# Splitting one 912-column load of a ReLU row-sum kernel into 112 + 8 + 8 partitions

## The chip, the cores and the metric

The kernel runs on one core of one Trainium2 chip. The metric is device time in microseconds (us). The kernel before takes 160.81 us (median of 6 runs, 160.70 to 160.96). A program on one core shows no second core to compare with, so I rely on repeated runs; every run quoted here was classed fast and the granted clock was 1.0.

## The reference

```python
x = np.random.randn(32, 512, 1024).astype(np.float32)
relu_x = np.maximum(x, 0)
return np.sum(relu_x, axis=-1).astype(np.float32)
```

That is 16,384 rows of 1,024 floats, 67.1 MB read once, and 16,384 sums written.

## The kernel before

Each of the 128 partitions takes 128 rows. Seven large chunks of 16 rows rotate through three buffers; then come 8, 4 and 2 rows, and the last two rows in pieces. ACT applies ReLU, DVE sums, and near the end both do ReLU and sum in one instruction each. All loads are issued by SP on one queue. The end of the load is cut into four transfers so that little computing is left after the last byte:

```python
CUT = 912
HEAD = 256
# ...
    rows = xv[-1].rearrange("p j d -> p (j d)")[:, r * D : (r + 2) * D]
    flat = buf[:, tb, r : r + 2, :].rearrange("p j d -> p (j d)")
    first, second, third = [(0, CUT), (D + D // 2, 2 * D), (D + HEAD, D + D // 2)]
    for k, (lo, hi) in enumerate((first, second, third)):
        sp.dma_start(out=flat[:, lo:hi], in_=rows[:, lo:hi]).then_inc(
            s_in[NBIG + len(TAIL) + k], 16
        )
    sp.dma_start(out=seam[:, 2 : 2 + w + HEAD], in_=rows[:, CUT : D + HEAD]).then_inc(s_seam, 16)
# ...
    lo, hi = first
    act.wait_ge(s_in[-3], 16)
    dve.wait_ge(s_in[-3], 16)
    on_act(flat[:, lo : CUT // 2], seam[:, 0:1]).then_inc(s_half, 1)
    on_dve(flat[:, CUT // 2 : hi], seam[:, 1:2]).then_inc(s_half, 1)
# ... then second (ACT), third (DVE), and the seam with the partial sums (both)
```

I call these four transfers the first piece (912 columns), the second (512), the third (256) and the seam (368). The result goes out after the last pair of instructions on the seam.

Of the kernel before, what the change touches and what calls it, by code (L numbers as in the profile page):

```python
# [3 lines left out]
P = 128  # L4
# [7 lines left out]
TAIL = [8, 4, 2]  # L12
CUT = 912
HEAD = 256


def bass_relu_sum_kernel(
# [21 lines left out]
    NBIG = len(CHUNKS)  # L39
# [12 lines left out]
    w = D - CUT  # L52
    seam = nc.alloc_sbuf_tensor("seam", [P, 2 + w + HEAD + 2], fp32)
    res = nc.alloc_sbuf_tensor("res", [P, J], fp32)
# [3 lines left out]
    s_in = [nc.alloc_semaphore(f"s_in{i}") for i in range(n_in)]  # L58
# [11 lines left out]
    sp, act, dve = nc.sync, nc.scalar, nc.vector  # L70
# [14 lines left out]
    for c in range(NBIG + 1):  # L85
        if c >= NB:
            sp.wait_ge(s_dve, done[c - NB])
        if c < NBIG:
            i = 0
            for g, j, n in CHUNKS[c]:  # L90
                sp.dma_start(  # L91
                    out=buf[:, c % NB, i : i + n, :], in_=xv[g][:, j : j + n, :]
# [15 lines left out]
    rows = xv[-1].rearrange("p j d -> p (j d)")[:, r * D : (r + 2) * D]  # L108
    flat = buf[:, tb, r : r + 2, :].rearrange("p j d -> p (j d)")
    first, second, third = [(0, CUT), (D + D // 2, 2 * D), (D + HEAD, D + D // 2)]  # L110
    for k, (lo, hi) in enumerate((first, second, third)):
        sp.dma_start(out=flat[:, lo:hi], in_=rows[:, lo:hi]).then_inc(  # L112
            s_in[NBIG + len(TAIL) + k], 16
        )
    sp.dma_start(out=seam[:, 2 : 2 + w + HEAD], in_=rows[:, CUT : D + HEAD]).then_inc(s_seam, 16)
    sp.wait_ge(s_turn, 1)
    sp.dma_start(
        out=of[0:P].rearrange("(k q) -> k q", q=32), in_=turned[0:P:32, 0:32]
# [7 lines left out]
    def on_act(t, acc):  # L126
        return act.activation(t, t, AF.Relu, accum_out=acc)  # L127

    def on_dve(t, acc):
        return dve.tensor_scalar(  # L130
            out=t, in0=t, scalar1=0.0, scalar2=None, op0=ALU.max, op1=ALU.add, accum_out=acc
        )
# [4 lines left out]
    k = 0  # L137
    for c in range(NTWO):
# [17 lines left out]
        for n in DVE_STEPS[c]:  # L156
            if ready[r + n - 1] > seen:
# [3 lines left out]
                out=res[:, c * BIG + r : c * BIG + r + n],  # L161
                in_=buf[:, c % NB, r : r + n, :],
# [22 lines left out]
            f(buf[:, tb, i, :], res[:, j0 + i : j0 + i + 1])  # L185

    lo, hi = first
    act.wait_ge(s_in[-3], 16)
    dve.wait_ge(s_in[-3], 16)
    on_act(flat[:, lo : CUT // 2], seam[:, 0:1]).then_inc(s_half, 1)  # L190
    on_dve(flat[:, CUT // 2 : hi], seam[:, 1:2]).then_inc(s_half, 1)
    k = 2 + w
    lo, hi = second
    act.wait_ge(s_in[-2], 16)
    on_act(flat[:, lo:hi], seam[:, k + HEAD : k + HEAD + 1]).then_inc(s_seam, 1)
    lo, hi = third
    dve.wait_ge(s_in[-1], 16)
    on_dve(flat[:, lo:hi], seam[:, k + HEAD + 1 : k + HEAD + 2]).then_inc(s_seam, 1)
    act.wait_ge(s_seam, 16 + 2)
    act.wait_ge(s_half, 2)  # L200
    on_act(seam[:, 0:k], res[:, J - 2 : J - 1]).then_inc(s_last, 1)
    dve.wait_ge(s_seam, 16 + 2)
    on_dve(seam[:, k : k + HEAD + 2], res[:, J - 1 : J]).then_inc(s_last, 1)

# [33 lines left out]
```

## Time and profile before

| | kernel before |
|---|---|
| median of 6 runs | 160.81 us |
| span of the profiled run | 159.4 us |
| DMA engines' share of the time, 20 to 120 us | 1.00 |
| bytes read | 67.11 MB |
| packet of 3,648 B (one row of the first piece) | 142 ns, one every 0.139 us |
| last landing of first piece, second, third, seam | 155.93, 156.63, 156.99, 157.44 us |
| start of the last pair of instructions | 157.47 us |

A transfer does not land at one time: the trace has 16 semaphore updates for each of these transfers, and from 153 to 157 us their packets run in 16 trains side by side, so I count one update from each DMA engine. A wait ends with the last of them (DVE's wait for the third piece at 157.01 us, the last landing at 156.99). The lines of the profile, and how I read them, are in the prediction.

### The profile page before, as it was taken

Reading aid. Unit: us, or ns where it says so; the run is one execution under the profiler, and the core shown is the slowest. Engines: PE = TensorE matmul, PEld = TensorE weight load, DVE = VectorE, ACT = ScalarE, POOL = GpSimd, SP = SyncE. Lnnn points to the kernel's source line nnn. Section 1 sums busy time; section 2 is a strip of 40 time slices with the busy share of each in tenths; the row PEclk is TensorE's granted clock in tenths of the full one; section 3 lists DMA queues with packets and bytes.
Section 4 is the critical chain, followed back from the end, with each engine's and each line's share of the span. In section 5 each row is a group of like instructions: output and inputs, shape, how many; then the busy total and the mean of one; then the engine's idle time right before and its main releaser. Section 6 shows DMA issues by size and latency. Waiting matters only on the chain.

```text
span 159.4 us, 150 instructions
## 1 busy us (share of the span) xinstructions
DVE 120.6 (76%) x59; ACT 101.5 (64%) x54; POOL 0.2 (0%) x4
## 2 busy tenths in 40 slices
DVE  0000000009999999999999999999999999898995
ACT  3000059980799708996099941999329980496975
POOL 0000000000000000000000000000000000000000
DMA  9997996996996997989979969969969979798994
GB/s 378 493 401 339 493 526 263 526 526 263 526 493 296 526 444 345 526 378 411 526 312 477 526 263 526 526 263 526 526 263 526 444 345 526 321 469 374 417 400 142
DMA packets 2457, 67.18 MB, mean 421 GB/s; under 512 B 536, under 2 KB 792, under 8 KB 1176
## 3 DMA queue, kind: packets, MB, share of 16 engines
q1 hardware_dynamic: 2456, 67.18, 98.1%
q14 instruction: 1, 0.01, 0.0%
HBM read 67.11 MB, written 0.07 MB: 421 GB/s over the span
## 4 chain that ended last, share of the span: by engine, by line
DVE 55%; DMA 34%; ACT 9%; SPq 2%; issue 0%
DVE res L160 54%; DMA buf<-in_x_dram 34%; ACT buf L145 9%; SPq L101 1%; SPq L112 1%; DVE buf L130 0%; DVE seam L130 0%; SPq L91 0%; DVE turned L169 0%
## 5 line engine op out<-in xcount | busy, mean ns | idle before, releaser
L160 DVE TENSOR_REDUCE res<-buf 128x4 f32<-128x4096 f32 (+3 forms) x18 | 99.4, 5596 | 35.5 <-ACT buf L145 35.5
L145 ACT ACTIVATE buf<-buf 128x7168 f32<-128x7168 f32 (+5 forms) x13 | 80.4, 6233 | 46.1 <-DMA buf<-in_x_dram 46.1
L127 ACT ACTIVATE buf<-buf 128x1024 f32<-128x1024 f32 (+2 forms) x19 | 19.0, 999 | 8.9 <-DMA buf<-in_x_dram 8.9
L130 DVE TENSOR_SCALAR_CACHE_REDUCE buf<-buf 128x1024 f32<-128x1024 f32 (+2 forms) x19 | 20.7, 1143 | 1.7 <-DMA buf<-in_x_dram 1.6
L127 ACT ACTIVATION_READ_ACCUMULATOR buf<-buf 128x1 f32 x19 | 3.6, 188 | 0.0
L145 ACT ACT_TABLE_LOAD x1 | 1.3, 1283 | 1.3 <-PEq L223 1.3
L130 DVE DVE_READ_ACCUMULATOR buf<-buf 128x1 f32 x19 | 1.6, 84 | 0.0
L130 DVE TENSOR_SCALAR_CACHE_REDUCE seam<-seam 128x258 f32<-128x258 f32 x1 | 0.4, 421 | 0.0
L127 ACT ACTIVATE seam<-seam 128x114 f32<-128x114 f32 x1 | 0.3, 300 | 0.1
L169 DVE STREAM_TRANSPOSE turned<-res 128x32 f32<-128x32 f32 x1 | 0.2, 211 | 0.0
L127 ACT ACTIVATION_READ_ACCUMULATOR seam<-seam 128x1 f32 x1 | 0.2, 186 | 0.0
L223 POOL MEMSET const-bfloat16-1.0<- 128x1 bf16 x1 | 0.1, 101 | 0.0
L223 POOL MEMSET const-uint8-127<- 128x1 uint8 x1 | 0.1, 101 | 0.0
L223 POOL MEMSET const-float32-0.0<- 128x1 f32 x1 | 0.1, 98 | 0.2 <-issue 0.2
L223 POOL MEMSET const-float32-1.0<- 128x1 f32 x1 | 0.1, 98 | 0.0
L130 DVE DVE_READ_ACCUMULATOR seam<-seam 128x1 f32 x1 | 0.1, 82 | 0.0
## 6 DMA issues: line engine op xcount, KB each, us to landing
buf<-in_x_dram SPq DMA_DIRECT2D x1, 7680.0 KB, 21.1
buf<-in_x_dram SPq DMA_DIRECT2D x1, 4096.0 KB, 25.3
buf<-in_x_dram SPq DMA_DIRECT2D x1, 2048.0 KB, 29.9
buf<-in_x_dram SPq DMA_DIRECT2D x1, 1024.0 KB, 31.9
buf<-in_x_dram SPq DMA_DIRECT2D x1, 512.0 KB, 3.3
buf<-in_x_dram SPq DMA_DIRECT2D x1, 456.0 KB, 32.5
buf<-in_x_dram SPq DMA_DIRECT2D x1, 256.0 KB, 32.7
seam<-in_x_dram SPq DMA_DIRECT2D x1, 184.0 KB, 32.6
```

Of the source, the lines that this page charges most:

```text
L101: sp.dma_start(out=buf[:, tb, r : r + n, :], in_=xv[-1][:, r : r + n, :]).then_inc(s_in[NBIG + i], 16)
L112: sp.dma_start(out=flat[:, lo:hi], in_=rows[:, lo:hi]).then_inc(s_in[NBIG + len(TAIL) + k], 16)
L127: return act.activation(t, t, AF.Relu, accum_out=acc)
L130: return dve.tensor_scalar(out=t, in0=t, scalar1=0.0, scalar2=None, op0=ALU.max, op1=ALU.add, accum_out=acc)
L145: act.activation(t, t, AF.Relu).then_inc(s_act, 1)
L160: dve.tensor_reduce(out=res[:, c * BIG + r : c * BIG + r + n], in_=buf[:, c % NB, r : r + n, :], axis=X, op=ALU.add,).then_inc(s_dve, 1)
L169: dve.transpose(out=turned[:, :], in_=res[:, 0:32]).then_inc(s_turn, 1)
L223: nc = _bacc.Bacc("TRN2", target_bir_lowering=False, num_devices=1)
```

## The change

The intent: eight of the engines finish earlier than the other eight (the first piece's eighth landing at 155.68 us, the last at 155.93), so let the early ones carry part of the late ones' rows. The large transfer puts 7 rows on each of sixteen engines and the small ones one row each on eight: eight engines carry 9 rows and eight carry 7, where each carried 8. The wait is for 48.

```diff
+SHARES = [(0, 112), (112, 120), (120, 128)]
...
     for k, (lo, hi) in enumerate((first, second, third)):
-        sp.dma_start(out=flat[:, lo:hi], in_=rows[:, lo:hi]).then_inc(
-            s_in[NBIG + len(TAIL) + k], 16
-        )
+
+        for a, b in SHARES if k == 0 else [(0, P)]:
+            sp.dma_start(out=flat[a:b, lo:hi], in_=rows[a:b, lo:hi]).then_inc(
+                s_in[NBIG + len(TAIL) + k], 16
+            )
...
-    act.wait_ge(s_in[-3], 16)
-    dve.wait_ge(s_in[-3], 16)
+    act.wait_ge(s_in[-3], 16 * len(SHARES))
+    dve.wait_ge(s_in[-3], 16 * len(SHARES))
```

## The prediction

- Step 5 came to 0.97 us more on the engines that carry the small transfers. The 0.97 was my estimate, and no trace shows it. From it follow the seam at 157.23 + 0.97 = 158.20 us, 0.76 us later, and 160.91 + 0.76 = 161.67 us. The forecast is the weighted sum, 0.6 x 0.76 - 0.4 x 0.06 = +0.43, rounded to +0.5: 161.4 us, with a range of 160.75 to 162.3. In the same way the 1.11 us expected of e4 and the doubling expected of e3 and e7 were estimates.
- "Port", "own port" and "crowded" are my names for choices of the partitions that a transfer writes. I supposed that some choices make the engines slow each other.
- "Engines 0 to 7" are the eight engines that carry the small transfers, "8 to 15" the other eight. No trace numbers the engines; these are names only.

> **What bounds the kernel now.** I read the share of the DMA engines by stage first, then the chain that ended last, then the end of the timeline, and last the landings in the trace.
>
> The stage table of the kernel before (columns: stretch in us, its length, busy time of DVE, ACT and POOL, clock, share of the 16 DMA engines, GB/s):
>
> ```profile
> 20.00:120.00 100.00, 84.47 (x16) 71.38 (x11) 0.00 (x0) 1.00 1.00 432
> ...
> 147.00:152.00 5.00, 4.57 (x8) 4.27 (x8) 0.00 (x0) 1.00 0.97 415
> 152.00:154.80 2.80, 2.45 (x6) 2.19 (x4) 0.00 (x0) 1.00 0.99 410
> 154.80:156.00 1.20, 1.16 (x3) 1.16 (x3) 0.00 (x0) 1.00 1.01 386
> 156.00:157.50 1.50, 1.07 (x7) 1.38 (x5) 0.00 (x0) 1.00 0.52 177
> ```
>
> The transfers hold their engines for practically the whole span until 156, while DVE and ACT have slack. The load is the bound. The chain's shares (DVE 55%, DMA 34%) mislead here: in the middle the chain runs along DVE because DVE frees the buffers, but the queue always has the next transfer waiting. So only two things could shorten the run: fewer or faster bytes, or a shorter end. The change aims at the end.
>
> The end of the chain of waits (start, length, what):
>
> ```profile
> 124.39 32.60 DMA buf<-in_x_dram
> 156.99 0.02 issue
> 157.01 0.44 DVE buf L130 x2
> 157.45 0.02 issue
> 157.47 0.43 DVE seam L130 x2
> ```
>
> and the timeline there:
>
> ```profile
> 155.96 0.58 ACT L127 ACTIVATE buf<-buf 128x456 f32<-128x456 f32 x1
> 155.98 0.08 DVE L130 DVE_READ_ACCUMULATOR buf<-buf 128x1 f32 x1
> 155.98 0.62 DVE L130 TENSOR_SCALAR_CACHE_REDUCE buf<-buf 128x456 f32<-128x456 f32 x1
> ...
> 156.65 0.63 ACT L127 ACTIVATE buf<-buf 128x512 f32<-128x512 f32 x1
> 157.01 0.42 DVE L130 TENSOR_SCALAR_CACHE_REDUCE buf<-buf 128x256 f32<-128x256 f32 x1 [0.40 <-DMA buf<-in_x_dram]
> ...
> 157.93 0.34 SPq L207 DMA_DIRECT2D out_dram<-res  x1
> ```
>
> What to see: DVE waits 0.40 us for the third piece, and the last pair (seam) starts at 157.47. From there the way to the end is fixed work: 0.43 us on DVE, the store issued at 157.93, its last landing at 159.35.
>
> The trace's semaphore updates tell what the page doesn't: each transfer lands in 16 steps, one per DMA engine. First, eighth, ninth and last step: 155.43, 155.68, 155.70, 155.93 us for the piece that is changed (912 columns); 156.49, 156.72, 156.78, 156.99 for the third; 156.98, 157.23, 157.25, 157.44 for the seam. So the engines run about 0.46 us apart, and 157.47 is set by three things almost at once: the seam's last landing at 157.44, the end of DVE's third piece at 157.45, and ACT's second piece ending at 157.38. Which engines are early? The 4-partition store of the transposed sums lands at 157.15, 157.22, 157.23, 157.32, which repeats the seam's four earliest steps (156.98, 157.04, 157.05, 157.14) 0.17 to 0.18 us later. Its engines are the four early ones.
>
> [...] 65,536 B rows take 2,418 ns per packet, 27.1 GB/s on one engine. [...]
>
> **The change part by part.**
>
> 1. *Compute: nothing changes.* The instruction order on DVE and ACT is the same, only line numbers move.
>
> 2. *SP: two more issues.* An issue on those lines takes 441 to 463 ns. Everything after the first piece is issued about 2 x 0.46 = 0.92 us later, so the seam at about 125.8 instead of 124.87. It starts moving at about 156. This is hidden by 30 us. Cost 0.
>
> 3. *Packets.* A 3,648 B packet shows 142 ns, and they follow each other every 0.139 us. The completion packet shifts the stream by some 0.006 us (one train goes on 145 ns instead of 139 after it). Before, each engine had 8 x 0.139 = 1.112 us of this piece. After, engines 8 to 15 have 7 packets (0.139 us less) and engines 0 to 7 have 9, with two more completions: 0.139 + 0.012 = 0.151 us more.
>
> 4. *What that is worth if each packet keeps its 0.139 us.* Third piece: late half 156.99 - 0.14 = 156.85, early half 156.72 + 0.15 = 156.87, so it lands 0.12 earlier. Seam: late half 157.44 - 0.14 = 157.30, early half 157.23 + 0.15 = 157.38, so 0.06 earlier. DVE's third piece then ends at about 157.33. ACT gains nothing: its 456-column half starts at 155.96 behind its own row before, and its second piece ends at 157.38 as now. So the last pair starts at about 157.41 instead of 157.47. **Best case: 0.06 us of 160.91, thus 160.85.** Most of the 0.139 us is not to be had.
>
> 5. *What it costs if ports are shared.* [...] Their seam would land at 157.23 + 0.97 = 158.20 instead of the 157.44 that sets the end now: 0.76 us later. **Port case: about 160.91 + 0.76 = 161.67.** The 112-partition transfer may add to it[...]. I can't size that from the trace; if a third of its packets took twice their time it would be 2 x 0.139 = 0.28 us, which gives 161.95.
>
> **The rivals.** (a) *It works as meant*, 160.85. For it: the 0.46 us stagger is there in every transfer, and the early engines are the ones that a transfer of 8 uses. [...] (b) *A crowded port becomes the bound of the last two microseconds*, 161.67 to 161.95. [...] Against: each small transfer has just 29 KB, and the crowding lasts only a moment. (c) *The gain is hidden anyway*: landings move up, but ACT's second piece at 157.38 or the seam keeps the last pair where it is; 160.9. It differs from (a) by less than the spread of the three runs (160.76 to 160.96). (d) *The two more issues delay a transfer*: the landings are 32.6 us behind their issue, so this costs nothing.
>
> **Range and chances.** I give (b) about 60%, (a) and (c) together 40%. Weighted: 0.6 x 0.76 - 0.4 x 0.06 = +0.43 us, less than either branch of (b), and I round it to +0.5: 161.4. The distribution has two humps, so the range covers both: from 160.75 (gain of 0.06 and the spread of runs) to 162.3 (port case, with a costly 112-partition transfer). Two per cent are 3.2 us. No mechanism that I found moves the time by that, because the part concerned lasts 1.1 us of transfer and all the work after the first crossing takes under 4 us. Faster by over 2% I put at 0.005, slower by over 2% at 0.02.
>
> **What would show it.** Step 1: the same instruction counts on DVE and ACT. Step 2: the seam issued near 125.8 and still moving first near 156. Step 3: 128 packets of 3,648 B as before, plus 16 more completion updates from engines for the two small transfers; if packets keep 142 ns, (a) holds. Steps 4 and 5: the third piece's last step at 156.87 means (a), near 157.7 means (b); its 16 steps come closer together in (a) and spread wider in (b). In (b) many of the 3,648 B packets should show well over 142 ns, and the DMA share of 156.00:157.50 should rise. The seam's last landing at 157.4 is (a) or (c), at 158.2 it is (b).
>
> The prediction would be wrong if the 112-partition transfer were spread over fewer engines than 16 (7 rows would become 14 or more on an engine, a microsecond or more), or if an engine switched badly between short transfers. Both would show as packet gaps after 154.

## The result, and the profile after

| | before | after |
|---|---|---|
| median of 6 runs | 160.81 us | 161.57 us |
| range | 160.70 to 160.96 | 161.47 to 161.75 |
| ratio, 95% interval | | 1.0048 (1.0035 to 1.0061) |
| last landing of first piece | 155.93 us | 156.69 us |
| last landing of the second, third | 156.63, 156.99 us | 157.31, 157.70 us |
| seam, first and last landing | 156.98, 157.44 us | 157.91, 158.16 us |
| mean time of a 3,648 B packet | 144 ns | 178 ns |
| mean time of a 2,048 B packet | 85 ns | 147 ns |

A ratio is the mean time of one kernel's fast runs over that of the other's fast runs of the same rounds, so it is not quite the ratio of the medians. The changed kernel is slower by 0.76 us by the medians: within 2%, but clear of the noise.

The stage table of the changed kernel, for the same three last stretches as before (stretch, length, busy time of DVE, ACT and POOL, clock, DMA share, GB/s):

```profile
152.00:154.80 2.80, 2.50 (x6) 2.19 (x4) 0.00 (x0) 1.00 1.01 407
154.80:156.00 1.20, 0.96 (x1) 0.96 (x1) 0.00 (x0) 1.00 1.06 245
156.00:157.50 1.50, 0.91 (x4) 0.98 (x5) 0.00 (x0) 1.00 1.00 309
```

Read the last two columns together. From 154.80 to 156.00 the engines are as busy as before (1.06; it was 1.01), yet they move 245 GB/s instead of 386. Busy engines with fewer bytes are engines whose packets take longer: the mean 3,648 B packet took 178 ns instead of 144. (A share a little over 1 can come from packet records that overlap; before, they were 142 ns long and 139 ns apart.) In the next stretch the work that was not done is still there: a DMA share of 1.00 instead of 0.52.

The end of the chain of waits of the changed kernel:

```profile
125.09 32.61 DMA buf<-in_x_dram
157.70 0.02 issue
157.72 0.44 DVE buf L133 x2
158.16 0.02 issue
158.19 0.43 DVE seam L133 x2
```

It has the same form as before (the line number moved from 130 to 133), with all of it 0.70 to 0.72 us later. And its timeline there:

```profile
156.71 0.58 ACT L130 ACTIVATE buf<-buf 128x456 f32<-128x456 f32 x1 [0.52 <-DMA buf<-in_x_dram]
156.71 0.63 DVE L133 TENSOR_SCALAR_CACHE_REDUCE buf<-buf 128x456 f32<-128x456 f32 x1 [0.45 <-DMA buf<-in_x_dram]
...
157.34 0.63 ACT L130 ACTIVATE buf<-buf 128x512 f32<-128x512 f32 x1
157.72 0.42 DVE L133 TENSOR_SCALAR_CACHE_REDUCE buf<-buf 128x256 f32<-128x256 f32 x1 [0.37 <-DMA buf<-in_x_dram]
...
158.64 0.34 SPq L210 DMA_DIRECT2D out_dram<-res  x1
```

Before, ACT and DVE started the two halves of the first piece at 155.96 and 155.98 with no wait shown, because they were still at work. Now both stand idle, 0.52 and 0.45 us, for the first piece. The seam's 16 landings are now 0.24 us apart instead of 0.46. So the change does level the engines, as it was meant to; it levels them at a later time.

### The profile page after: what moved, and what is told of

Read it like the earlier page. It is cut to its first block, busy times and chain, and to the rows that moved or that the text cites. A ratio compares the mean times of both kernels' runs of the same rounds, so it can differ in the third digit from the quotient of the medians.

```text
span 160.1 us, 152 instructions
## 1 busy us (share of the span) xinstructions
DVE 120.7 (75%) x59; ACT 101.5 (63%) x54; POOL 0.2 (0%) x4
## 2 busy tenths in 40 slices
DMA packets 2473, 67.18 MB, mean 420 GB/s; under 512 B 552, under 2 KB 808, under 8 KB 1192
## 4 chain that ended last, share of the span: by engine, by line
DVE 55%; DMA 34%; ACT 9%; SPq 2%; issue 0%
DVE res L163 54%; DMA buf<-in_x_dram 34%; ACT buf L148 9%; SPq L115 1%; SPq L102 1%; DVE buf L133 0%; DVE seam L133 0%; SPq L92 0%; DVE turned L172 0%
```

## The experiments

My theory, called the **port theory** in the expectations: what costs the time is which partitions the rows go to, since with some choices the engines slow each other. What the runs can test is whether the destination counts. The main rival, the **load theory**: the time comes from what the engines carry, from nine rows on eight of them or from transfers that run on eight engines only. A third: more and shorter transfers cost time as such.

A profile of one run can be off by 0.1 us and more before the end is even reached: the last landing of the 2,048 KB transfer, the second ahead of the first piece, came anywhere from 152.29 to 152.63 us in these runs. So beside the medians I give the **tail**: the seam's last landing less that landing, which the first piece does not touch yet. It is 157.44 - 152.30 = 5.14 us in the kernel before and 158.16 - 152.36 = 5.80 us in the changed one, +0.66.

| kernel | rows of 912 columns by engine (the eight that take more, the other eight) | median | before, same rounds | ratio (95%) | tail against 5.14 |
|---|---|---|---|---|---|
| changed kernel | 9, 7 | 161.57 | 160.81 | 1.0048 (1.0035 to 1.0061) | +0.66 |
| e1: 112 + 16 | 8, 8 | 161.82 | 160.81 | 1.0056 (1.0044 to 1.0068) | +0.82 |
| e2: three column slices | 8, 8 | 160.96 | 160.81 | 1.0007 (0.9995 to 1.0019) | +0.08 |
| e3: 64 + 64 | 8, 8 | 162.03 | 160.81 | 1.0072 (1.0060 to 1.0084) | +1.20 |
| e6: small ones spread | 9, 7 | 161.69 | 160.81 | 1.0049 (1.0037 to 1.0061) | +0.74 |
| e5: extra, every 4th from 0 | 10, 8 | 160.92 | 160.79 | 1.0011 (0.9997 to 1.0025) | +0.09 |
| e7: extra, every 4th from 64 | 10, 8 | 161.21 | 160.79 | 1.0025 (1.0012 to 1.0037) | +0.31 |
| e4: extra, 112 to 127 | 10, 8 | 161.74 | 160.79 | 1.0058 (1.0045 to 1.0070) | +0.85 |
| e8: large one as changed | 9, 7 | 161.12 | 160.83 | 1.0018 (1.0006 to 1.0031) | +0.35 |
| e9: small ones as changed | 9, 7 | 161.33 | 160.83 | 1.0031 (1.0018 to 1.0045) | +0.47 |
| e10: neither | 9, 7 | 160.77 | 160.83 | 0.9994 (0.9982 to 1.0007) | -0.09 |

### e1: the same large transfer with an even load

```diff
-SHARES = [(0, 112), (112, 120), (120, 128)]
+SHARES = [(0, 112), (112, 128)]
```

> The changed piece as 112 partitions and then 16 partitions, both over all sixteen engines: every engine has 7 + 1 rows, so the load is even again and no transfer runs on eight engines. Port theory [...]: still slower than before by 0.4 to 0.9 us, with many 3,648 B packets near 200 ns as in the changed kernel. Load theory (engines 0 to 7 with nine rows, or the transfers on eight engines, cost the time): within 0.1 us of before and packets of 142 ns.

Measured: 161.82 us, +1.01 by the medians, somewhat over the 0.4 to 0.9 that I expected (the tail, +0.82, lies within it). That is more than the changed kernel, though the two intervals overlap. In the stretch from 154.80 on, busy engines again move little:

```profile
154.80:156.00 1.20, 0.85 (x1) 0.85 (x1) 0.00 (x0) 1.00 0.99 264
```

93 of the 128 packets of 3,648 B took over 155 ns, against 82 in the changed kernel and 4 before. Every engine has eight rows here and no transfer runs on eight engines (2,473 DMA packets against 2,457 before: 16 completion packets more for the one transfer more). So neither the nine rows nor the eight-engine transfers are needed for the loss; the load theory falls as the explanation of it.

### e2: three transfers that keep all 128 partitions

```diff
-SHARES = [(0, 112), (112, 120), (120, 128)]
+SHARES = [(0, 304), (304, 608), (608, 912)]
...
-            sp.dma_start(out=flat[a:b, lo:hi], in_=rows[a:b, lo:hi]).then_inc(
+            sp.dma_start(out=flat[:, a:b], in_=rows[:, a:b]).then_inc(
```

(with the loop's other case changed to the whole column range)

> The piece as three transfers of 304 columns each, always 128 partitions: two more issues and two more completions per engine[...]. Port theory: 0 to +0.1 us against before. Theory that more and shorter transfers cost the time: +0.3 to +0.8 us.

Measured: 160.96 us, +0.15 by the medians, with an interval that includes 1 and ends at 1.0019, which is 0.3 us. The tail grew by 0.08 us. 1,216 B packets took 53 ns, hardly one more than that, and the stretch shows no fall in what is moved:

```profile
154.80:156.00 1.20, 1.07 (x3) 0.89 (x2) 0.00 (x0) 1.00 1.09 399
```

Two more transfers on this path may cost something like 0.1 us; they do not explain 0.76.

### e3: two transfers of 64 partitions

```diff
-SHARES = [(0, 112), (112, 120), (120, 128)]
+SHARES = [(0, 64), (64, 128)]
```

> The piece as two transfers of 64 partitions, each over sixteen engines with four rows: load even, no small transfers[...]. Port theory: packets near 2 x 139 = 278 ns and +1.1 us at the end (the piece takes 2.2 us instead of 1.1)[...]. Load theory: 0, packets 142 ns.

Measured: 162.03 us, +1.22, the slowest of all, with an even load (2,473 DMA packets, so 16 completions for each half). The median 3,648 B packet took 248 ns, against 142 before and the 278 that I expected. The stretch:

```profile
154.80:156.00 1.20, 0.73 (x1) 0.73 (x1) 0.00 (x0) 1.00 1.00 227
```

227 GB/s is 0.59 of the 386 that the kernel before moved there. What changed is which partitions a transfer covers (and one transfer became two, which by e2 costs little), and the price is close to the +1.1 us expected. That figure rested on packets of double length, which was my estimate; why 64 partitions cost this, the run does not show.

### e6: the same unequal load, small transfers spread

```diff
-SHARES = [(0, 112), (112, 120), (120, 128)]
+SHARES = [slice(0, 96), slice(96, 128, 2), slice(97, 128, 4), slice(99, 128, 4)]
```

(with the loop changed to take these slices)

> The same unequal load as the changed kernel (nine rows on engines 0 to 7, seven on the others), but the small transfers take every fourth partition [...]: 96 partitions, 16 (every second), 8 and 8 (every fourth). Port theory: the part of the slowdown that the small transfers cause goes, so +0.2 to +0.6 us against before[...]. Load theory: as the changed kernel, +0.75 us or more. If it comes out at or above +0.75, the misaligned large transfer is the cause and not the small ones.

Measured: 161.69 us, +0.88 by the medians and the same ratio as the changed kernel. I had expected 0.2 to 0.6. By the rule that I wrote down, this points to the large transfer rather than to the small ones. But it is a poor test: the small rows, though spread, still go to partitions 96 to 127, the large transfer now has 96 partitions, and a fourth transfer (16 rows, every second partition) joined them. The run alone settles nothing about which transfer is to blame, so I built e8 to e10 for that.

### e5, e7, e4: the same bytes and engines, three destinations

These add two needless transfers (8 rows x 912 columns each) to the kernel before, from the same source rows. Each run has 2,489 DMA packets, 32 more than before: 16 rows and 16 completions, so eight engines for each transfer. Only the partitions that they write, in a tensor that nobody reads, differ. The results stay right.

```diff
+    spare = nc.alloc_sbuf_tensor("spare", [P, CUT], fp32)
...
+        for q, a in EXTRA if k == 0 else []:
+            sp.dma_start(out=spare[q, 0:CUT], in_=rows[a : a + 8, lo:hi]).then_inc(s_extra, 16)
...
+EXTRA = [(slice(0, 32, 4), 112), (slice(1, 32, 4), 120)]           # e5
+EXTRA = [(slice(64, 96, 4), 112), (slice(65, 96, 4), 120)]         # e7
+EXTRA = [(slice(112, 120), 112), (slice(120, 128), 120)]           # e4
```

(and a wait on `s_extra` at the very end; the constants of the three runs stand side by side here)

> The same two needless transfers, the same source rows and bytes, but into partitions 0, 4, ... 28 and 1, 5, ... 29 of the spare tensor[...]. Both theories: engines 0 to 7 lose 0.29 us, of which 0.21 lies in the stagger, so +0.08 us against before and packets of 142 ns. If it is as slow as the crowded one, ports are not the cause.

> The same two needless transfers into partitions 64, 68, ... 92 and 65, 69, ... 93[...]. Port theory: [...] the end moves by about +0.28 us (early half 157.23 + 2 x 0.278 = 157.79, +0.35): between the own ports and the crowded ones. Load theory: +0.08 us, as for the own ports. It also tests whether early engines can take over anything for late ones[...].

> The kernel before plus two needless transfers of 8 rows x 912 columns on engines 0 to 7, into partitions 112 to 119 and 120 to 127 of a spare tensor: the large transfers stay as before. Port theory: [...] engines 0 to 7 lose 1.11 us, their seam lands at 157.23 + 1.11 = 158.34 and the end moves by +0.9 us ([...] over +0.4 in any case). Load theory: engines 0 to 7 move two packets more, 0.278 + 0.012 us, seam at 157.52, end +0.08 us.

The stretch from 154.80 to 156.00, first for e5:

```profile
154.80:156.00 1.20, 1.16 (x3) 1.16 (x3) 0.00 (x0) 1.00 1.00 389
```

for e7:

```profile
154.80:156.00 1.20, 1.08 (x1) 1.08 (x2) 0.00 (x0) 1.00 1.04 335
```

and for e4:

```profile
154.80:156.00 1.20, 1.18 (x2) 1.15 (x2) 0.00 (x0) 1.00 1.07 293
```

389, 335, 293 GB/s: nothing but the destination partitions moved. The tails are +0.09, +0.31 and +0.85 us against expected +0.08, +0.28 to +0.35 and +0.9 (by the medians +0.13, +0.42 and +0.95). This is the plainest evidence that what counts is where the rows land. e5 and e7 even have the same step of four partitions and differ only in the partitions that they start from (0 and 1 against 64 and 65): 389 against 335 GB/s. e7 also says something about the intent: rows that the early engines carry are not free for the late ones. Measured from the 2,048 KB transfer, rank by rank, the last eight landings of e7's first piece came 0.17 to 0.29 us later than in the kernel before, the first eight 0.01 to 0.18 us. So early engines take over little in e7.

e4 shows that the delay does not stay with the engines that make the extra writes. Eight engines make them; yet in e4 even the first landing of the seam, 157.83 us, comes after its last landing in the kernel before, 157.44, so no engine was spared. By what way the delay reaches the others, no run here shows. Nor does it show in the 3,648 B packets: they ended by 155.57 us (155.45 before), while the first piece, the same transfer as before and ahead of the extra ones, landed last at 156.49 (155.93 before).

e5 shows one more thing. Its seam lands first at 157.22, 0.24 us later than before, and last at 157.52, 0.08 later. The eight engines of the extra rows, the only ones with more work, are thus the early ones, which the prediction had taken for granted.

### e8, e9, e10: one destination at a time

All three give each engine the bytes of the changed kernel. Their results are wrong, since the small transfers go to the spare tensor. (The comparison with the reference passed them all the same, presumably because few sums are touched and the stale columns are of similar size.)

```diff
-        for a, b in SHARES if k == 0 else [(0, P)]:
+        n, c = LARGE if k == 0 else (P, hi)
+        sp.dma_start(out=flat[0:n, lo:c], in_=rows[0:n, lo:c]).then_inc(
...
+        for q, a in SMALL if k == 0 else []:
+            sp.dma_start(out=spare[q, 0:CUT], in_=rows[a : a + 8, lo:hi]).then_inc(
...
+LARGE = (112, 912); SMALL = [(slice(0, 32, 4), 112), (slice(1, 32, 4), 120)]    # e8
+LARGE = (128, 798); SMALL = [(slice(112, 120), 112), (slice(120, 128), 120)]    # e9
+LARGE = (128, 798); SMALL = [(slice(0, 32, 4), 112), (slice(1, 32, 4), 120)]    # e10
```

(and the wait on the piece for all of its transfers, as in the changed kernel; the constants side by side again)

> Wrong result on purpose (the piece of partitions 112 to 127 goes into a spare tensor). The 112-partition transfer of the changed kernel as it is, and its two small transfers with the same bytes and engines but into every fourth partition of the spare tensor[...]. Bytes per engine as in the changed kernel. [...] If the large one is the main cause: +0.5 to +0.8 us against before. If it is the small ones: -0.1 to +0.2 us.

> Wrong result on purpose. The large transfer as 128 partitions x 798 columns, the same bytes as 112 x 912 [...]; the two small transfers into partitions 112 to 119 and 120 to 127 (of a spare tensor). Bytes per engine as in the changed kernel. [...] If they are enough: +0.5 to +0.8 us (my estimate of 0.97 us on engines 0 to 7 puts the seam's last landing 0.76 us later). If the large one is the cause: -0.1 to +0.2 us. If both this and the run with the large one alone are slow, the two overlap and do not add, since the changed kernel is only 0.76 us slower.

> Wrong result on purpose. The large transfer as 128 partitions x 798 columns and the two small ones into every fourth partition of the spare tensor[...], with the changed kernel's bytes per engine: what the change was meant to do, without crowding. Port theory with the early half on engines 0 to 7: -0.06 us (seam's last landing 0.06 earlier against the landings before the piece, and its 16 steps closer together, about 0.25 us instead of 0.46). Load theory: as slow as the changed kernel, +0.75 us.

The stretch for e8:

```profile
154.80:156.00 1.20, 1.04 (x1) 1.04 (x2) 0.00 (x0) 1.00 1.01 285
```

for e9:

```profile
154.80:156.00 1.20, 1.14 (x1) 1.14 (x2) 0.00 (x0) 1.00 1.08 262
```

and for e10:

```profile
154.80:156.00 1.20, 1.07 (x1) 1.07 (x2) 0.00 (x0) 1.00 1.01 388
```

e10 has the load of the change without either of its two destinations: 388 GB/s (386 before), packets of 142 ns, the 16 landings of the seam 157.46 - 157.16 = 0.30 us apart. Its time is 0.06 us under the kernel before by the medians, and its tail 0.09 shorter. The interval includes 1, so no gain is shown, but a gain of 0.06 us could not be told from none by these rounds. The loss, though, is gone, with the same load on every engine.

e8 puts the cost of the large transfer at +0.29 us and e9 that of the small ones at +0.50 us, by the medians. Both fit neither of the two simple answers that I had set up ("the large one, +0.5 to +0.8" or "the small ones"): e8 falls between them, e9 just reaches its range. The causes are two. Counted from e10 they are 0.29 + 0.06 = 0.35 and 0.50 + 0.06 = 0.56 us, in sum 0.91; the changed kernel stands 0.76 + 0.06 = 0.82 above e10. So by the medians they nearly add. By the tails, 0.44 and 0.56 us above e10 against 0.75 for the changed kernel, they overlap by a quarter of a microsecond. With intervals of about 0.2 us each way on every ratio, and one profile for each tail, these runs can't decide it. One rival is also left for the large transfer: it changes not only where an engine writes but also which source rows it reads. e5, e7 and e4 rule the source out for the small transfers; for the large one no run tests the destination alone.

Where each shows is worth seeing. In e8 the 3,648 B packets themselves took longer (181 ns in the mean). In e9 the small transfers' own 16 packets took 146 ns in the mean; it is the 2,048 B packets queued behind them that took 153 ns instead of 85. A packet's record does not have to be long where the queue was caused; the next packets may be.

A version faster than both kernels does not follow. e10 is no valid kernel, and to make it one, moved rows would have to be summed in other partitions with further instructions, for 0.06 us at best.

## Why the prediction was right or wrong

**The bound, the path to the end, compute.** Right, with two slips in the readings that cost nothing. DVE has no slack in the middle: from 35.5 to 120 us it is busy for 84.47 of 84.50 us. That the load is the bound rests on the DMA share of about 1.00 alone. And the engines are not 0.46 us apart in every transfer: the prediction's own landings give 0.50, 0.50 and 0.46 us. DVE and ACT have the same instructions (59 and 54), and the end is the same chain, 0.72 us later, with the same 1.9 us of work behind it.

**Step 2, issues.** Right that it is hidden; the size was off. The seam was issued at 125.56, 0.69 us later and not 0.92, since the issues of 8 partitions took 0.39 and 0.27 us. Its first packet moved at 156.88 us instead of 156.04, later because the pieces ahead of it were. Something unforeseen happened on SP, told below; it was hidden as well.

**Step 3, packets.** The counts were right: 128 packets of 3,648 B, and 292 completion packets instead of 276, the 16 more that were expected. Their duration was not the 142 ns of the intended case.

**Step 4, the best case.** It did not come about, but e10 made it on purpose and gave -0.06 us by the medians, which is the number worked out. With an interval of 0.2 us each way so close a match is luck; the run shows that the loss is gone, not the gain. That most of the 0.139 us can't be had, because the early half comes to the fore and ACT is not waiting, fits that run.

**Step 5, the port case.** That the destinations cost the time is what the runs show, and the total was near: +0.76 us forecast and +0.76 measured by the medians, the seam's last landing at 158.20 and at 158.16. But so good a fit is luck, for the split was off. The step put all 0.76 us on the two small transfers and left the large one as an addition that could not be sized (+0.28, a guess of one packet in three at double time). Measured, the small ones alone cost 0.50 us (e9) and the large one alone 0.29 (e8). The step's term for the small transfers, an estimate, was too large in e9, where it gave 0.76, yet in e4, with an unchanged first piece ahead, it held: the end was to move by 0.9 and the tail grew by 0.85. Why it holds in the one and not in the other stays open. The step also let only the eight engines of the small transfers lose time, while in e4, as told above, no engine was spared, and in the changed kernel neither: the seam's first landing, 157.91 us, comes after the last one before, 157.44. The guess for the large one came out at the right size with the wrong picture: 82 of 128 packets, not a third, took over 155 ns, at about 200 ns and not at double time. A total that fits thus came from one term too large and one left out.

**The rivals.** (b) was right in its time, with its 60%; what makes these destinations slow, no run shows. (a) is refuted for this kernel by its own signs: packets did not keep 142 ns. (c) fell as well, since the last pair starts 0.72 us later. (d), the issues, cost nothing that the end could show. Weighting (b) against (a) gave 161.4, and the measured 161.57 lies inside the range of 160.75 to 162.3, nearer to the 161.67 of (b) itself.

**The signs named beforehand.** The third piece's last landing "near 157.7": 157.70. The DMA share of 156.00 to 157.50 "should rise": 0.52 to 1.00. One sign was wrong: in case (b) the third piece's 16 landings were to spread wider, but they came closer, 0.29 us apart instead of 0.50 (the seam's 0.24 instead of 0.46). The unequal load alone brings them together: in e10, without the two destinations, the seam's are 0.30 us apart. The prediction gave this sign to (a) alone, but the load is as unequal in (b).

## What to carry to other kernels

Before a transfer is cut by partitions to balance DMA engines, look at which partitions its rows go to. Each cut of the piece by partitions that was tried here (112 + 8 + 8, 112 + 16, 64 + 64, 96 + 16 + 8 + 8) cost 0.76 to 1.22 us; the cut by columns, with all 128 partitions in each transfer, moved the median by 0.15 us, with an interval that includes 1 (e2). A stagger of half a microsecond between engines is not what levelling can bring: the working gave 0.06 us, and e10 could not show even that. And in these runs, where the DMA share stayed near 1.0 while GB/s fell, the destinations made the difference: vary them first.

## What the runs showed besides

- A transfer of 112 partitions also runs on sixteen engines (7 rows each, as told under The change), yet e8, with only this transfer cut, lost 0.29 us on a transfer of about 1.1 us and moved 285 GB/s where e10 moved 388. The runs show the cost for 112 (e8) and 64 partitions (e3), not its cause.
- The 16 landings of one load issued by SP lie apart: 0.46 to 0.53 us in the last six loads of the kernel before, with the eight engines that carry the extra rows of e5 ahead.
- One issue on SP took long while loads were still under way. The store of the transposed sums was issued in 0.63 us with 8 loads not yet landed (before) and with 9 (e1 and e3); with 10 it took 8.37 us in the changed kernel and 21.92 us in e2. The count alone does not explain it, since no load landed between 126.0 us and the end of the wait at 134.4 in the changed kernel. It is harmless here only because SP has nothing more to issue until about 157 us. The changed kernel's timeline has it as

```profile
126.04 8.37 SPq L120 DMA_DIRECT2D out_dram<-turned  x1
```
